# Uniform operand offsets, the attention mask as a TensorE product, and softmax scaling on ScalarE

## The chip, the cores and the metric

The kernel runs on one core of a Trainium2 chip. The metric is device time in microseconds (us) of the whole kernel, the median of three runs. TensorE (PE in the profile; PEld is its weight load) does the products, VectorE (DVE) and ScalarE (ACT) do element-wise work, GpSimd (POOL) some of it and a few transfers, SyncE (SP) issues the others.

## The reference

The reference is one layer of a diffusion block for 256 latent and 256 context tokens of width 2048. Cut to what matters:

```python
h  = modulate(rms_norm(x, norm_attn_w), sh_a, sc_a)        # shift, scale and gate come from silu(c) @ w_ada + b_ada
hc = modulate(rms_norm(ctx, norm_attn_w), csh_a, csc_a)
q, k, v, u = split_projection(h @ w_in)                     # 16 query heads, 4 key heads of 64
qc, kc, vc, uc = split_projection(hc @ w_in)
# latent window attention: each query sees latent keys at most 128 away, all 256 context keys and a sink logit
s_win = where(abs(qpos - kpos) <= 128, q @ k.T / 8, -1e30)
p = softmax(concat([s_win, q @ kc.T / 8, sink]))            # the sink's share is dropped
attn = p_win @ v + p_ctx @ vc
x = x + g_a * (concat([attn, multiscale_pool(u)]) @ w_out)
hm = modulate(rms_norm(x, norm_mlp_w), sh_m, sc_m)
x = x + g_m * (square(relu(hm @ w_mlp_up)) @ w_mlp_down)    # hidden width 8192
out = rms_norm(x, final_norm_w)
```

All data are float32.

## The kernel before

Every large product is split in two parts per operand: hi is the operand rounded to the type fp32r, lo is the rest. `mm3` adds three products (hi x hi, hi x lo, lo x hi) in one bank of PSUM. Weights come in tiles of 128 x 2048 numbers through a ring of five buffers (`raw`, class `WeightStream`); `split_to` makes their parts in halves of 128 x 1024: ScalarE casts `hi`, VectorE subtracts `lo`, in rings of six. The activations have the same two parts: `hhi` and `hlo` for the input projection (`modulated`), `mx` (both parts in one tile) for the output projection and the up product, `ahi` and `alo` for the down product (`activation`). The line of a product in the profile is that of `mm3` (290, 291, 292), of `up_group` (920) or of the attention.

The stages follow each other: modulation and input projection (to about 207 us), attention with the last input projections, the pooling mixer and some modulation products (`ps_ada`) mixed in (207 to about 315), output projection (`ps_w`), norm, then the MLP in turns: two up groups (`ps_up`), then a down stretch (`ps_d`).

Attention goes through 16 units: a pair of heads and a block of 128 queries. The 512 keys of a unit are 256 latent and 256 context keys. For each of its two heads, `scores` makes a bank of 128 x 512 scores by two products; the mask concerns 128 of its columns. `maxima` adds the mask on VectorE and takes the row maxima; `exponentials` makes the exponentials and their sums on ScalarE; `normalize` adds the sink's share to the sums, inverts them and scales the probabilities `p` on VectorE; `transpose` turns `p` on TensorE (`tp_p`) and ScalarE copies the result to `pT`; `attend` multiplies it with the values (`ps_o`). The loop writes, for step n: scores of unit n, `attend`, transposes of unit n - 2, maxima of n, normalization of n - 1, exponentials of n. A scheduler then sets each engine's order from that program; each engine runs its own list strictly in that order and waits at its head.

`gap` allocates a few bytes that nothing uses, so that the tiles behind it begin elsewhere. The places below are the first byte of a tile in each partition of SBUF, as a remainder by 512 (128 float32 numbers, one row of a weight tile of 128 columns).

Of the kernel before, what the change touches and what calls it, by code (L numbers as in the profile page):

```python
# [9 lines left out]
F32R = mybir.dt.float32r  # L10
I32 = mybir.dt.int32
AF = mybir.ActivationFunctionType
ALU = mybir.AluOpType
AX = mybir.AxisListType

P = 128
# [33 lines left out]
def gap(pool, n, name="gap"):  # L50

    pool.tile([P, n // 4], F32, tag=name, name=name, bufs=1)


class WeightStream:
# [28 lines left out]
    def split_to(self, n):  # L88
        nc = self.nc
        while self.n_half < min(n, len(self.halves)) and not self.hold:  # L90
            i, h = self.halves[self.n_half]
            if i >= self.n_load:
                break
            raw = self.raw[i][:, 2 * h : 2 * h + 2, :]
            hi = self.pool.tile([P, 2, 512], F32R, tag="hi", name="hi", bufs=N_HALF)
            if not self.n_half:
                gap(self.pool, 320)
            lo = self.pool.tile([P, 2, 512], F32R, tag="lo", name="lo", bufs=N_HALF)
            up = nc.scalar.copy(hi, raw)  # L99
            low = nc.vector.tensor_tensor(lo, raw, hi.bitcast(F32), ALU.subtract)  # L100
            self.last = (up.ins, low.ins)
            self.split[i, h] = (hi, lo)
            self.n_half += 1
# [23 lines left out]
def kernel(  # L127
# [314 lines left out]
    def modulated(c_, streams=(0, 1)):  # L442

        pool = hpb if c_ in (2, 3, 6, 7) else hpa
        if 0 in streams:
            hhi = pool.tile([P, 2, 512], F32R, tag="hhi", name="hhi", bufs=2)
            if c_ in (0, 2):
                gap(pool, 320, "gaph")
            hlo = pool.tile([P, 2, 512], F32R, tag="hlo", name="hlo", bufs=2)
            hparts[c_] = hhi, hlo  # L450
        hhi, hlo = hparts[c_]
        for j in range(2):
            k = 2 * c_ + j
            xk = xT[k // 4][:, k % 4, :]
            for s in streams:
                v = xk[:, T * s : T * s + T]
                nc.vector.tensor_scalar(v, v, am_a[:, k, s : s + 1], sm_a[:, k, s : s + 1], ALU.mult, ALU.add)
            ts_ = slice(T * streams[0], T * streams[-1] + T)
            up = nc.scalar.copy(hhi[:, j, ts_], xk[:, ts_])
            low = nc.vector.tensor_tensor(hlo[:, j, ts_], xk[:, ts_], hhi[:, j, ts_].bitcast(F32), ALU.subtract)  # L460
            hs[k] = lambda s, j=j: (hhi[:, j, s], hlo[:, j, s])
        return up.ins, low.ins
# [122 lines left out]
    for op in in_ops:  # L585
        if op[0] == "ctx":
            with tc.issue_after(first_split[0]), tc.issue_after(first_split[1]):
                normalize(2)
                normalize(3)
            modulated(0, (1,))  # L590
            xn_es.close()
            mixa = ctx.enter_context(tc.tile_pool(name="mixa", bufs=1, side="left", reuse_waits="tile"))
            gap(mixa, 192)
            hpb = hpb_es.enter_context(tc.tile_pool(name="hpb", bufs=1, side="left", reuse_waits="tile"))
            gap(hpb, 192)
        else:
            run_in(op)
    gap(hpa, 320)
    st_es.close()
    hpa_es.close()  # L600

# [5 lines left out]
    def parts(j):  # L607
# [17 lines left out]
                            fill=MASKED, base=0, channel_multiplier=1)  # L625
    nc.gpsimd.affine_select(out=mask[:, 1, :], in_=mask[:, 1, :], pattern=[[1, P]], compare_op=ALU.is_ge,
                            fill=MASKED, base=0, channel_multiplier=-1)

    swap = [(i + 16) % 32 for i in range(32)]

# [76 lines left out]
    class Unit:  # L707
# [4 lines left out]
        def scores(self):  # L712
            khi, klo = kparts[self.cc // 2]
            self.s = []
            for i in range(2):
                ps = bank("ps_s")
                q = qparts[self.cc, i][:, P * self.qb : P * self.qb + P]
                nc.tensor.matmul(ps, q, khi, start=True, stop=False)
                nc.tensor.matmul(ps, q, klo, start=False, stop=True)
                self.s.append(ps)  # L720

        def maxima(self):

            st = atp.tile([P, 4, 2], F32, tag="st", name="st", bufs=6)
            mx, self.sum, self.es, self.nm = (st[:, i, :] for i in range(4))
            for i, ps in enumerate(self.s):
                far = ps[:, P : 2 * P] if self.qb == 0 else ps[:, 0:P]
                nc.vector.tensor_tensor(far, far, mask[:, self.qb, :], ALU.add)
                nc.vector.reduce_max(mx[:, i : i + 1], ps, axis=AX.X)
            nc.vector.scalar_tensor_tensor(self.nm, mx, -0.125, nsink[:, self.heads], ALU.mult, ALU.min)  # L730
            nc.vector.tensor_tensor(self.es, sink[:, self.heads], self.nm, ALU.add)
# [8 lines left out]
        def normalize(self):  # L740
            nc.vector.tensor_tensor(self.sum, self.sum, self.es, ALU.add)
            nc.vector.reciprocal(self.sum, self.sum)
            for i in range(2):
                p = self.p[:, i, :]
                nc.vector.tensor_scalar(p, p, self.sum[:, i : i + 1], None, ALU.mult)

        def transpose(self):
            if self.qb == 0:
# [49 lines left out]
    for n in range(len(units) + 3):  # L798
        if n < 16:
            if n % 4 == 0:  # L800
                split_keys(n // 4)
            units[n].scores()
        fill_to((n + 0.5) / 17)
        if n >= 4 and n % 2 == 0:
            attend((n - 4) // 2)
        if 2 <= n < 18:
            units[n - 2].transpose()
        if n < 16:
            units[n].maxima()
        if 1 <= n < 17:  # L810
            units[n - 1].normalize()
        if n < 16:
            units[n].exponentials()
            if n % 2 == 0 and n < 14:
                split_queries(n // 2 + 1)
        fill_to((n + 1) / 17)
# [71 lines left out]

    def activation(pss):
        ahi = mp.tile([P, 4, T], F32R, tag="ahi", name="ahi", bufs=3)  # L890
        gap(mp, 64)
        alo = mp.tile([P, 4, T], F32R, tag="alo", name="alo", bufs=3)
        for m in range(4):
            t = mp.tile([P, T], F32, tag="act", name="act", bufs=2)
            if pss[m].shape[1] == T:
                nc.scalar.activation(t, pss[m], AF.Relu)
                nc.vector.tensor_tensor(t, t, t, ALU.mult)
            else:
                nc.scalar.copy(t, pss[m][:, T : 2 * T])
                nc.vector.tensor_tensor(t, pss[m][:, 0:T], t, ALU.add)  # L900
                nc.vector.scalar_tensor_tensor(t, t, 0.0, t, ALU.max, ALU.mult)
            nc.scalar.copy(ahi[:, m, :], t)
            nc.vector.tensor_tensor(alo[:, m, :], t, ahi[:, m, :].bitcast(F32), ALU.subtract)
        return ahi, alo
# [198 lines left out]
```

## Time and profile before

| | us |
|---|---|
| median of three runs | 1156.07 (1155.22 to 1157.96) |
| the profiled execution, whole | 1154.18 |
| its span, from the first to the last instruction | 1152.4 |
| TensorE busy | 1109.2 (96%) |
| VectorE busy | 801.9 (70%) |
| ScalarE busy | 504.9 (44%) |
| GpSimd busy | 35.5 (3%) |

Busy shares are averages over stages with different limits. A TensorE product is counted until its modelled end, so products in close order overlap, and the distance of their starts says more than their duration. A line such as `out<-in` names the tiles of an instruction without buffer numbers; `x` is a count.

### The profile page before, as it was taken

To read this page: it belongs to the slowest core of one execution; us is meant where nothing else is said; L and a number is where in the kernel's file an instruction comes from. 1 tells how busy PE (TensorE), PEld (TensorE's weight loads), DVE (VectorE), ACT (ScalarE), POOL (GpSimd) and SP (SyncE) were. 2 spreads that over 40 slices of the span, in tenths; PEclk is the share of its full clock that TensorE was granted. 3 is DMA by queue.
4 is the path that set the end of the run, shared out by engine and by line. 5 is a ranking of instruction groups with operands and counts; after the bars stand their busy time and mean duration, and the time that the engine had idled before them with its cause. 6 is when DMAs were issued, how large, how long until landed. Compare 5 with 4: busy or idle time off the path is not lost.

```text
span 1152.4 us, 16086 instructions
## 1 busy us (share of the span) xinstructions
PE 1109.2 (96%) x6332; PEld 903.4 (78%) x6332; DVE 801.9 (70%) x1286; ACT 504.9 (44%) x762; POOL 35.5 (3%) x53
## 2 busy tenths in 40 slices
PE   4999999979999989999999999999999999999996
PEld 3767778746578869988888888888888888888885
DVE  5655557988787888796775774784664665587576
ACT  4623233377634443365433444433444443443452
POOL 1000001610000000000000000000000000000000
PEclk9999999999999989999999999999999999999998
DMA  9999897667897999977775775676556556556532
GB/s 341 358 342 345 274 332 265 212 237 272 278 380 266 311 324 343 354 257 248 272 247 184 255 268 197 239 260 205 186 189 200 192 183 184 192 188 203 183 110 74
DMA packets 174012, 286.66 MB, mean 249 GB/s; under 512 B 5608, under 2 KB 72352, under 8 KB 172784
## 3 DMA queue, kind: packets, MB, share of 16 engines
q1 hardware_dynamic: 172800, 279.55, 72.4%
q0 software_dynamic: 848, 5.55, 1.3%
q8 instruction: 50, 0.82, 0.3%
q10 hardware_dynamic: 288, 0.52, 0.1%
q14 instruction: 26, 0.21, 0.1%
HBM read 283.50 MB, written 2.10 MB: 248 GB/s over the span
## 4 chain that ended last, share of the span: by engine, by line
PE 80%; DVE 9%; DMA 6%; ACT 2%; issue 1%; SPq 0%; POOL 0%; ACTq 0%; DVEq 0%
PE ps_up L920 25%; PE ps_d L290 10%; PE ps_d L291 10%; PE ps_d L292 10%; PE ps_ada L307 5%; DMA raw<-in_w_mlp_up_dram 3%; DVE lo L100 3%; PE ps_qu L290 2%; PE ps_qu L292 2%; PE ps_qu L291 2%; DVE ada_v L329 1%; PE ps_o L764 1%; PE ps_w L290 1%; PE ps_w L292 1%; PE ps_w L291 1%
## 5 line engine op out<-in xcount | busy, mean ns | idle before, releaser
L100 DVE TENSOR_TENSOR lo<-raw,hi 128x1024 fp32r<-128x1024 f32 x330 | 396.9, 1224 | 210.4 <-ACT hi L99 203.8
L99 ACT CAST hi<-raw 128x1024 fp32r<-128x1024 f32 x330 | 337.7, 1050 | 414.5 <-PE ps_up L920 150.6
L290 PE MATMUL ps_d<-hi,ahi 128*128 128x512 f32 (+1 forms) x520 | 202.8, 391 | 0.0
L291 PE MATMUL ps_d<-lo,ahi 128*128 128x512 f32 (+1 forms) x520 | 202.3, 390 | 0.0
L920 PE MATMUL ps_up<-mx,hi 128*128 128x512 f32 x832 | 200.0, 392 | 0.0
L292 PE MATMUL ps_d<-hi,alo 128*128 128x512 f32 (+1 forms) x520 | 199.8, 388 | 0.0
L920 PEld LDWEIGHTS ps_up<-mx,hi 128*128 128x128 f32 x832 | 153.4, 188 | 31.8 <-issue 1.9
L292 PEld LDWEIGHTS ps_d<-hi,alo 128*128 128x128 f32 x520 | 97.7, 188 | 22.4
L290 PEld LDWEIGHTS ps_d<-hi,ahi 128*128 128x128 f32 x520 | 97.8, 188 | 21.7
L291 PEld LDWEIGHTS ps_d<-lo,ahi 128*128 128x128 f32 x520 | 97.7, 188 | 20.7
L329 DVE SCALAR_TENSOR_TENSOR ada_v<-raw,c_sil,ada_v 128x512 f32<-128x512 f32 x135 | 100.8, 747 | 14.7 <-DMA raw<-in_w_ada_dram 13.1
L920 PEld LDWEIGHTS ps_up<-mx,lo 128*128 128x128 f32 x832 | 105.3, 189 | 4.0
L920 PE MATMUL ps_up<-mx,lo 128*128 128x256 f32 x832 | 106.6, 281 | 0.0
L307 PE MATMUL ps_ada<-raw,c_sil 128*32 128x512 f32 x480 | 70.8, 625 | 0.9 <-DMA raw<-in_w_ada_dram 0.9
L290 PE MATMUL ps_qu<-hhi,hi 128*128 128x256 f32 x240 | 69.8, 292 | 1.4 <-ACT hi L99 1.4
L292 PE MATMUL ps_qu<-hhi,lo 128*128 128x256 f32 x240 | 67.4, 284 | 0.3 <-DVE lo L100 0.3
L291 PE MATMUL ps_qu<-hlo,hi 128*128 128x256 f32 x240 | 67.3, 281 | 0.0
L290 PEld LDWEIGHTS ps_qu<-hhi,hi 128*128 128x128 f32 x240 | 45.4, 189 | 16.6 <-issue 9.2
L290 PE MATMUL ps_up<-mx,hi 128*128 128x256 f32 x192 | 54.0, 290 | 1.6 <-ACT mx L885 1.5
L291 PE MATMUL ps_up<-mx,hi 128*128 128x256 f32 x192 | 53.5, 283 | 0.0
L292 PE MATMUL ps_up<-mx,lo 128*128 128x256 f32 x192 | 52.4, 283 | 0.0
L290 PE MATMUL ps_w<-hi,mx 128*128 128x512 f32 x128 | 51.4, 402 | 0.0
(199 smaller groups left out, 1323.1 us busy)
## 6 DMA issues: line engine op xcount, KB each, us to landing
raw<-in_w_ada_dram SPq DMA_DIRECT2D x128, 512.0 KB, 7.5
raw<-in_w_mlp_up_dram SPq DMA_DIRECT2D x64, 1024.0 KB, 5.4
raw<-in_w_mlp_down_dram SPq DMA_DIRECT2D x64, 1024.0 KB, 5.1
raw<-in_w_ada_dram SPq DMA_DIRECT2D x32, 1024.0 KB, 6.2
raw<-in_w_in_dram SPq DMA_DIRECT2D x19, 1024.0 KB, 7.6
raw<-in_w_out_dram SPq DMA_DIRECT2D x16, 1024.0 KB, 7.8
xnat<-in_x_dram SPq DMA_DIRECT2D x2, 1024.0 KB, 6.0
xnat<-in_ctx_dram SPq DMA_DIRECT2D x2, 1024.0 KB, 11.6
```

The source lines that it names most:

```text
L99: up = nc.scalar.copy(hi, raw)
L100: low = nc.vector.tensor_tensor(lo, raw, hi.bitcast(F32), ALU.subtract)
L290: nc.tensor.matmul(ps, a[0], b[0], start=first, stop=False, skip_group_check=True)
L291: nc.tensor.matmul(ps, a[0], b[1], start=False, stop=False, skip_group_check=True)
L292: nc.tensor.matmul(ps, a[1], b[0], start=False, stop=last, skip_group_check=True)
L307: nc.tensor.matmul(ps[32 * j : 32 * j + 32, :], c_sil[:, 4 * kg + j, :], raw[:, j, :], start=(kg == 0), stop=(kg == 3), tile_position=(0, ...
L329: nc.vector.scalar_tensor_tensor(box["e"], raw[:, j, :], sc, box["e"], ALU.mult, ALU.add)
L764: nc.tensor.matmul(ps[64 * i : 64 * i + 64, 0:T], va[k // 2][:, k % 2, 64 * g : 64 * g + 64], pT[:, k, i, :], start=(k == 0), stop=(k == 3 ...
L920: nc.tensor.matmul(ps, wk, h, start=part == k == 0, stop=part == 1 and k == KC - 1, skip_group_check=True)
```

## The change

Offsets. The gaps between `hi` and `lo`, between `hhi` and `hlo`, and in front of `mx` go; the gap between `ahi` and `alo` moves behind `alo`. `hhi` and `hlo` get one tag for each of their two buffers, in the same turn as before. The places change so (remainder by 512):

| tile | before | after |
|---|---|---|
| `hi` (weights) | 160 | 160 |
| `lo` (weights) | 480 | 160 |
| `hhi` | 352 | 352 |
| `hlo` | 160 | 352 |
| `mx` | 160 | 160 |
| `ahi` | 416 | 416 |
| `alo` | 480 | 416 |

In the down product `hi` and `lo` are streamed (the moving operand) and `ahi` and `alo` are the weights loaded into the array; in the up product it is the other way, `mx` is streamed and `hi` and `lo` are loaded. By 2048 the remainder of `mx` goes from 1696 to 1184, that of `hi` is 1184 in both.

Mask. Two copies in fp32r, `mask_r` and `ident_r`, are made once on ScalarE. Behind the two score products a third one, identity times mask, adds the mask to its 128 columns of the bank; VectorE's add is gone. Normalization: the probabilities are scaled by ScalarE. The loop writes the normalization of unit n - 1 ahead of the maxima of unit n.

```diff
@@ split_to
             hi = self.pool.tile([P, 2, 512], F32R, tag="hi", name="hi", bufs=N_HALF)
-            if not self.n_half:
-                gap(self.pool, 320)
             lo = self.pool.tile([P, 2, 512], F32R, tag="lo", name="lo", bufs=N_HALF)
@@ modulated
-            hhi = pool.tile([P, 2, 512], F32R, tag="hhi", name="hhi", bufs=2)
-            if c_ in (0, 2):
-                gap(pool, 320, "gaph")
-            hlo = pool.tile([P, 2, 512], F32R, tag="hlo", name="hlo", bufs=2)
+            hhi = pool.tile([P, 2, 512], F32R, tag=f"hhi{c_ % 2}", name="hhi", bufs=1)
+            hlo = pool.tile([P, 2, 512], F32R, tag=f"hlo{c_ % 2}", name="hlo", bufs=1)
@@ pools
-            gap(mixa, 192)
...
-    gap(hpa, 320)
+    gap(hpa, 128)
@@ masks
+    mask_r = atp.tile([P, 2, P], F32R, name="mask_r")
+    ident_r = atp.tile([P, P], F32R, name="ident_r")
+    nc.scalar.copy(mask_r, mask)
+    nc.scalar.copy(ident_r, ident)
@@ scores
-                nc.tensor.matmul(ps, q, khi, start=True, stop=False)
-                nc.tensor.matmul(ps, q, klo, start=False, stop=True)
+                nc.tensor.matmul(ps, q, khi, start=True, stop=False, skip_group_check=True)
+                nc.tensor.matmul(ps, q, klo, start=False, stop=False, skip_group_check=True)
+                far = ps[:, P : 2 * P] if self.qb == 0 else ps[:, 0:P]
+                nc.tensor.matmul(far, ident_r, mask_r[:, self.qb, :], start=False, stop=True, skip_group_check=True)
@@ maxima
-                far = ps[:, P : 2 * P] if self.qb == 0 else ps[:, 0:P]
-                nc.vector.tensor_tensor(far, far, mask[:, self.qb, :], ALU.add)
@@ normalize
-                nc.vector.tensor_scalar(p, p, self.sum[:, i : i + 1], None, ALU.mult)
+                nc.scalar.activation(p, p, AF.Copy, scale=self.sum[:, i : i + 1])
@@ the loop over units
+        if 1 <= n < 17:
+            units[n - 1].normalize()
         if n < 16:
             units[n].maxima()
-        if 1 <= n < 17:
-            units[n - 1].normalize()
@@ activation
         ahi = mp.tile([P, 4, T], F32R, tag="ahi", name="ahi", bufs=3)
+        alo = mp.tile([P, 4, T], F32R, tag="alo", name="alo", bufs=3)
         gap(mp, 64)
-        alo = mp.tile([P, 4, T], F32R, tag="alo", name="alo", bufs=3)
```

The scheduler's lists of the two kernels differ in the attention stage and in a few places of the output projection and norm; the order of transfers is the same.

VectorE, second and third unit (the second unit's probabilities are `p_2231`, the third's `p_2325`; their small columns are `st_2220` and `st_2314` before, `st_2226` and `st_2320` after; `ps_s_2263` and `ps_s_2266` or `ps_s_2267` are the third unit's scores), before:

```order
L728 TENSOR_TENSOR ps_s_2263<-ps_s_2263,mask_1825 128x128
L728 TENSOR_TENSOR ps_s_2266<-ps_s_2266,mask_1825 128x128
L741 TENSOR_TENSOR st_2220<-st_2220 128x2
L729 TENSOR_REDUCE st_2314<-ps_s_2263 128x1
L729 TENSOR_REDUCE st_2314<-ps_s_2266 128x1
L742 RECIPROCAL st_2220<-st_2220 128x2
L438 TENSOR_TENSOR ua3_278<-ps_qu_2269,ua3_278 128x2x256
L730 SCALAR_TENSOR_TENSOR st_2314<-st_2314,nsink_1823 128x2
L745 TENSOR_SCALAR p_2231<-p_2231,st_2220 128x512 x2
```

and after:

```order
L740 TENSOR_TENSOR st_2226<-st_2226 128x2
L728 TENSOR_REDUCE st_2320<-ps_s_2263 128x1
L728 TENSOR_REDUCE st_2320<-ps_s_2267 128x1
L741 RECIPROCAL st_2226<-st_2226 128x2
L729 SCALAR_TENSOR_TENSOR st_2320<-st_2320,nsink_1819 128x2
L730 TENSOR_TENSOR st_2320<-sink_1817,st_2320 128x2
L436 TENSOR_TENSOR ua3_278<-ps_qu_2271,ua3_278 128x2x256
L740 TENSOR_TENSOR st_2320<-st_2320 128x2
L741 RECIPROCAL st_2320<-st_2320 128x2
```

(Line numbers of the changed kernel are one or two lower here.) The third unit's mask adds and the second unit's scalings are gone from this list. The second unit's reciprocal still stands behind the third unit's two maxima, and the third unit's own reciprocal now follows within a few rows.

ScalarE, a little later (`p_2325` as above, `p_2376` is the fourth unit's; `pT_2301` before and `pT_2303` after is the transposed copy of the first two units, `tp_p` the banks it empties), before:

```order
L737 ACTIVATE p_2325,st_2314<-ps_s_2263,st_2314 128x512
L737 ACTIVATE p_2325,st_2314<-ps_s_2266,st_2314 128x512
L755 COPY pT_2301<-tp_p_2302 128x4x128
L755 COPY pT_2301<-tp_p_2308 128x4x128
L735 ACTIVATE st_2314<-st_2314 128x2
L660 CAST qs0_2446<-qa1_272 64x256
L648 CAST khi_2649<-ka1_280 64x512
L649 CAST khi_2649<-ka1_280 64x512
L660 CAST qs1_2449<-qa1_272 64x256
L313 COPY ada_e_2404<-ps_ada_2212 128x512
L755 COPY pT_2301<-tp_p_2353 128x4x128
L755 COPY pT_2301<-tp_p_2359 128x4x128
```

and after:

```order
L754 COPY pT_2303<-tp_p_2304 128x4x128
L754 COPY pT_2303<-tp_p_2310 128x4x128
L659 CAST qs0_2446<-qa1_272 64x256
L744 ACTIVATE p_2325<-p_2325,st_2320 128x512 x2
L647 CAST khi_2649<-ka1_280 64x512
L648 CAST khi_2649<-ka1_280 64x512
L659 CAST qs1_2449<-qa1_272 64x256
L736 ACTIVATE p_2376,st_2371<-ps_s_2340,st_2371 128x512
L736 ACTIVATE p_2376,st_2371<-ps_s_2344,st_2371 128x512
L754 COPY pT_2303<-tp_p_2355 128x4x128
L734 ACTIVATE st_2371<-st_2371 128x2
L754 COPY pT_2303<-tp_p_2361 128x4x128
```

The scalings of the third unit (`p_2325<-p_2325`) are new here, and those of the second stand a few rows further up; both pairs come ahead of the last copies into `pT`, and the fourth unit's exponentials do too.

TensorE, from the second unit's transposes to the first product with the values (`ps_s_2392` and its partner are scores of the fifth unit, `ps_o` the product with the values), before:

```order
L307 MATMUL ps_ada_2212<-raw_2126,c_sil_75 32x512 x4
L307 MATMUL ps_ada_2212<-raw_2213,c_sil_75 32x512 x4
L753 MATMUL tp_p_2353<-ident_64,p_2231 128x128 x4
L753 MATMUL tp_p_2359<-ident_64,p_2231 128x128 x4
L718 MATMUL ps_s_2392<-khi_2386,qs0_2329 128x512
L719 MATMUL ps_s_2392<-klo_2387,qs0_2329 128x512
L718 MATMUL ps_s_2395<-khi_2386,qs1_2332 128x512
L719 MATMUL ps_s_2395<-klo_2387,qs1_2332 128x512
L764 MATMUL ps_o_2406<-pT_2301,va0_281 64x256
```

and after:

```order
L305 MATMUL ps_ada_2214<-raw_2128,c_sil_75 32x512 x3
L752 MATMUL tp_p_2355<-ident_64,p_2231 128x128 x4
L752 MATMUL tp_p_2361<-ident_64,p_2231 128x128 x4
L305 MATMUL ps_ada_2214<-raw_2128,c_sil_75 32x512
L717 MATMUL ps_s_2392<-khi_2386,qs0_2329 128x512
L718 MATMUL ps_s_2392<-klo_2387,qs0_2329 128x512
L720 MATMUL ps_s_2392<-mask_r_1829,ident_r_1830 128x128
L717 MATMUL ps_s_2396<-khi_2386,qs1_2332 128x512
L718 MATMUL ps_s_2396<-klo_2387,qs1_2332 128x512
L720 MATMUL ps_s_2396<-mask_r_1829,ident_r_1830 128x128
L305 MATMUL ps_ada_2214<-raw_2215,c_sil_75 32x512 x4
L763 MATMUL ps_o_2408<-pT_2303,va0_281 64x256
```

One product with the mask stands directly behind each pair of score products, and some of the modulation products (`ps_ada`) that stood ahead of the transposes stand behind them and behind the scores.

## Rows read from the trace of the kernel before

**Rows 1.** The page: busy time by engine; slices of TensorE and its clock.

```profile
PE 1109.2 (96%) x6332; PEld 903.4 (78%) x6332; DVE 801.9 (70%) x1286; ACT 504.9 (44%) x762; POOL 35.5 (3%) x53
...
PE   4999999979999989999999999999999999999996
...
PEclk9999999999999989999999999999999999999998
```

**Rows 2.** Attention by windows: us, busy (x count) by engine, TensorE clock, DMA share, GB/s.

```profile
222.00:242.00 20.00, 14.32 (x99) 8.80 (x97) 19.75 (x45) 11.40 (x30) 9.60 (x12) 1.00 0.58 215
242.00:262.00 20.00, 18.67 (x118) 8.76 (x118) 16.96 (x50) 14.42 (x35) 0.00 (x0) 1.00 0.70 231
262.00:282.00 20.00, 20.00 (x145) 12.84 (x144) 17.84 (x54) 15.13 (x41) 0.00 (x0) 1.00 0.69 250
282.00:309.00 27.00, 26.09 (x175) 15.35 (x170) 20.78 (x55) 20.32 (x47) 0.00 (x0) 1.00 0.77 270
207.00:309.00 102.00, 93.06 (x631) 58.03 (x632) 89.99 (x231) 64.04 (x159) 19.54 (x23) 1.00 0.67 235
```

**Rows 3.** TensorE's waits from 200 to 320: us in total, times, longest.

```profile
PE ps_o L764 <- ACT pT L755: 3.4, 2, 2.5
PE tp_p L753 <- DVE p L745: 3.2, 2, 1.8
...
PE tp_p L753 <- ACT pT L755: 0.8, 1, 0.8
```

**Rows 4.** Timeline of TensorE, 225 to 243; idle before and releaser in brackets.

```profile
225.61 1.09 PE L753 MATMUL tp_p<-ident,p 128*128 128x128 f32 x8
...
231.24 0.63 PE L753 MATMUL tp_p<-ident,p 128*128 128x128 f32 x4 [1.76 <-DVE p L745]
...
236.72 0.65 PE L764 MATMUL ps_o<-pT,va 128*64 128x256 f32 x2 [2.53 <-ACT pT L755]
...
242.87 0.30 PE L753 MATMUL tp_p<-ident,p 128*128 128x128 f32 x1 [1.48 <-DVE p L745]
```

**Rows 5.** Timeline of TensorE: start and end of a down stretch.

```profile
831.03 0.75 PE L920 MATMUL ps_up<-mx,lo 128*128 128x256 f32 x5
831.63 0.40 PE L290 MATMUL ps_d<-hi,ahi 128*128 128x512 f32 x1
...
876.01 1.30 PE L920 MATMUL ps_up<-mx,hi 128*128 128x512 f32 x5
```

**Rows 6.** Windows for one line: a down stretch (line 290), the up stretch behind it (line 920).

```profile
831.63:876.01 44.38, 25.27 (x64) 11.91 (x64) 1.00 0.60 188
...
876.01:920.31 44.30, 44.30 (x256) 39.11 (x255) 1.00 0.59 192
```

**Rows 7.** The page's costliest groups: count, busy us, mean ns, idle before.

```profile
L290 PE MATMUL ps_d<-hi,ahi 128*128 128x512 f32 (+1 forms) x520 | 202.8, 391 | 0.0
L291 PE MATMUL ps_d<-lo,ahi 128*128 128x512 f32 (+1 forms) x520 | 202.3, 390 | 0.0
...
L292 PE MATMUL ps_d<-hi,alo 128*128 128x512 f32 (+1 forms) x520 | 199.8, 388 | 0.0
```

**Rows 8.** VectorE's groups by line: count, busy us, mean ns, idle before.

```profile
L745 DVE TENSOR_SCALAR p<-p,st 128x512 f32<-128x512 f32 x32 | 15.1, 512 | 0.2
...
L728 DVE TENSOR_TENSOR ps_s<-ps_s,mask 128x128 f32<-128x128 f32 x32 | 8.7, 292 | 4.7 <-PE ps_s L719 4.4
```

**Rows 9.** Tiles `st` and `p`: ns min/median/max.

```profile
L730 DVE SCALAR_TENSOR_TENSOR st<-st,nsink x16: 147/151/2057, 215.4 to 300.0; 128x2 f32<-128x2 f32 x16
...
L745 DVE TENSOR_SCALAR p<-p,st x32: 472/480/1480, 223.1 to 304.3; 128x512 f32<-128x512 f32 x32
```

**Rows 10.** Line 1029: ns min/median/max.

```profile
L1029 ACT ACTIVATE x<-x,rs_y x5: 705/707/722, 1141.9 to 1146.8; 128x512 f32<-128x512 f32 x5
```

**Rows 11.** The chain that ended last, 200 to 320: start, us, step.

```profile
228.68 1.98 DVE st L730
```

**Rows 12.** Windows for line 745 (VectorE's scalings).

```profile
222.00:242.00 20.00, 3.66 (x6) 1.00 0.58 215
```

## Prediction

> **What bounds the kernel now.** I read the page's busy shares and slices first: TensorE is busy for 1109.2 of 1152.4 us, almost every slice from the second on shows a 9 for it, and its granted clock is at full speed nearly throughout [rows 1]. So time can come off in two ways only: TensorE's products follow each other more closely, or its few waits go. The table by stretches then shows where waits are possible: in the attention stage, 207 to 309 us, TensorE is busy for 93.06 of 102 us, and the shortfall lies mostly in 222 to 242 (14.32 of 20), where VectorE is busy for 19.75 of 20 [rows 2]. From 242 on TensorE is nearly full (18.67, 20.00, 26.09 of 20, 20 and 27). The list of waits names them: TensorE waited 3.2 us for the normalized probabilities from VectorE, 3.4 us for the transposed ones from ScalarE, 0.8 us for a bank that ScalarE was emptying, 7.4 us in all [rows 3]. The timeline has the three long ones, at 231.24, 236.72 and 242.87 [rows 4]. Everything after the stage is products in close order: a down stretch takes 876.01 - 831.63 = 44.38 us [rows 5] and holds 64 products of each of three kinds [rows 6], so 44.38 / 192 = 231 ns for each product of 512 columns. The next up stretch is 44.30 us for 256 products, 128 of 512 columns and 128 of 256 [rows 6]; five of the latter begin 831.63 - 831.03 = 0.60 us before the down stretch, so 0.12 us each [rows 5], which leaves (44.30 - 128 x 0.12) / 128 = 0.226 us for one of 512 columns.
>
> **Part 1: the offsets.** Nothing is computed differently; only tiles lie elsewhere. The direct hint is in the three lines of the down products: mean 391 ns (hi times ahi), 390 (lo times ahi), 388 (hi times alo) [rows 7]. The ends are modelled, but the three differ by the same rule. The third kind is the one whose follower streams from the same offset (hi, then the next hi); behind the first two the streamed operand jumps between 160 and 480. After the change all three stay at 160, and the weights loaded meanwhile lie at 416 throughout, as behind the third kind now. I take the third kind's duration for all three: 3 + 2 = 5 ns a triple, 520 triples [rows 7], 2.6 us less. Bounds: no gain, if the 3 ns belong to the place in the triple and not to the address; at best the up stretch's pace, (231 - 227) ns x 1560 = 6.2 us; at worst all three at the slowest line, 1 + 3 = 4 ns x 520 = 2.1 us more. In the up groups the lo weights move from 480 to 160. The hi weights of the same groups already lie at 160 with the streamed activations at 160, and these are the fastest products of 512 columns above, so I take nothing there; bounds 3 ns either way on 832 products, 2.5 us. The input and output projections (some 1,400 products) change in the same way; I have no row that sets their kinds apart, so nothing, with the smaller difference above as a bound, 1 ns each, 1.4 us.
>
> A rule speaks against this part: the Trainium skill (TensorE: Matmul & The Clock Gate, Step-by-step: what each phase is for) has two independent read ports for streamed operand and weights, so that loading the next weights takes no read bandwidth from the running product. By it addresses would not matter and this part's sum would be 0; the trace has only the 3 ns of 391 against it, and that rule is the reason for the third rival.
>
> **Part 2: mask on TensorE.** 32 products of 128 columns are added, one behind each pair of score products (the order shows it directly behind them). Nearest row: eight transposes of 128 columns took 1.09 us, 0.136 each with the last one's tail [rows 4]; from below, a quarter of a 512-column product, 231 / 4 = 58 ns. I take 0.11, nearer to the transposes, since they too load 128 columns of weights for 128 streamed: 32 x 0.11 = 3.5 us (1.9 to 4.4), on TensorE, which is the bound behind 242. VectorE loses 32 adds of 292 ns [rows 8]. The two copies that make the mask and identity operands stand once on ScalarE, well before the scores, where the stage before leaves it idle: nothing.
>
> **Part 3: normalization on ScalarE.** VectorE loses 32 x 0.51 = 16.3 us by the mean of its line, and 15.1 by its busy time [rows 8]. These instructions were also stretched: the median is 480 ns, the longest 1480, and the small instruction that makes the exponents' bias has 151 and 2057 [rows 9], while GpSimd worked on the pooling in the same stretch (9.60 of 20 us in 222 to 242 [rows 2]). ScalarE gains 32 scalings; the nearest row is its scaling of 512 columns by a column of scalars at the end of the kernel, 707 ns [rows 10]: 22.6 us. Here too a rule speaks against the change: the Trainium skill (ScalarE: Activation LUTs, Rules for kernel authors) sends multiplications to VectorE. By engine time the rows agree, 707 against 480 ns; by which engine is late in 222 to 242 they do not.
>
> What this does to the waits. Up to the reciprocal of the second unit VectorE drops six mask adds (6 x 0.29) and a pair of scalings (2 x 0.47), 2.7 us, and the chain of waits has the third unit's bias there, 1.98 us for a small instruction, on VectorE as well [rows 11]. So the second unit's probabilities come 4 us or more earlier, and TensorE's waits for VectorE (3.2) and for the bank (0.8) go: 4.0 us. The wait at 236.72 for ScalarE's transposed copy mostly stays: ScalarE starts earlier, but in the changed order it has two pairs of scalings (4 x 0.707 = 2.8 us) ahead of that copy; I take 0.9 off the 3.4. Behind 242 ScalarE is short: it is busy 14.42 + 15.13 + 20.32 = 49.87 of 67 us [rows 2], idle 17.1, and gets the scalings that VectorE now does from there on, 32 - 6 [rows 12], so 26 x 0.707 = 18.4. TensorE can run ahead a little, because the next transposes are two units behind, and the splits of the output weights can slip into the next stage; I put 1.0 us of new waits there.
>
> **Part 4: sums ahead of the next maxima.** This is written order only; in the built order the reciprocal of the second unit still stands behind the third's maxima, which no longer wait for mask adds. Nothing beyond part 3. DMA engines are at 0.58 to 0.77 in this stage [rows 2], so earlier consumption can be fed.
>
> **Sum.** Offsets -2.6; waits -4.0 - 0.9; mask products +3.5; new waits +1.0: -3.0 us. The profiled execution took 1154.18 us, 1.78 outside its span and 1.89 below the median of the three runs; on it the sum gives 1151.2, on the median 1156.07 - 3.0 = **1153.1 us**. A measurement of this kernel can tell about 0.2% (2.3 us) from no change.
>
> **Rivals.**
> *ScalarE becomes the bound (ends slower).* In 242 to 309 it would need 49.87 + 18.4 = 68.3 us of 67 without any waiting. If half of its former idle time was waiting for exponents' biases and products that still come in turn, 8.6 us, the stretch grows by 1.3 + 8.6 = 9.9 us, which hides the 26 mask products in it; with the earlier waits gone (-4.9) and six mask products in front (+0.7) the stage is 5.7 us longer, with the offsets' -2.6 the kernel +3.1: 1159.2. It decides from about 8 us of such waiting on. For it: the sum of busy times. Against: the splits can slip, and ScalarE waited because VectorE was late.
> *Equal offsets cost (slower).* Now streamed operand and weights meet at one offset in more pairs: +2.1 in the down groups, +2.5 in the up groups, attention -0.4: +4.2, 1160.3. For it: a tile's offset may matter either way. Against: the up groups' hi products.
> *The offsets do nothing (no change).* Only attention's -0.4 is left: 1155.7. For it: 3 ns of 391 is little, and the order within the triple could make it.
> *More of both (faster).* The down products fall to the up groups' pace (-6.2), all 7.4 us of waits go, mask products +3.5: -10.1, 1146.0.
>
> **How the numbers follow.** Forecast 0.31, more of both 0.14, offsets do nothing 0.28, ScalarE bound 0.19, equal offsets cost 0.08. The forecast lies 0.7 us beyond the bound of 2.3, so I put 0.23 of it under faster and 0.08 under no change. Of "offsets do nothing" 0.06 go to faster, 0.19 to no change, 0.03 to slower; of the two slower ones, 3.1 and 4.2 us above the median, 0.15 and 0.06 to slower, 0.04 and 0.02 to no change. That makes faster 0.23 + 0.14 + 0.06 = 0.43, same 0.33, slower 0.24. The range takes in the rivals at both ends as far as 8 in 10 need: 1146 to 1159.5; the forecast's own is 1150 to 1156.
>
> **What would show it.** Right: a down stretch of 192 products near 44.0 us instead of 44.38; TensorE's waits for probabilities gone in 222 to 243 and those for the transposed copy left; ScalarE nearly without idle time in 242 to 309; the first output product 0 to 1 us earlier than now. Wrong: down stretches unchanged or longer; TensorE waiting for ScalarE by several us behind 242; mask products that stand 0.2 us apart or delay the weights behind them.

## The result, and the profile after

The changed kernel takes 1147.05 us (median of five runs, 1143.71 to 1149.24), the kernel before 1155.8 in the same comparison (five runs, 1153.46 to 1157.96). The ratio is 0.9924, with an interval of 0.9904 to 0.9945: 8.8 us less, between 6.4 and 11.1. Forecast were 3.0 less.

The page of the changed kernel, the lines that answer to [rows 1]:

```profile
PE 1104.6 (96%) x6364; PEld 909.3 (79%) x6364; DVE 779.2 (68%) x1222; ACT 523.6 (46%) x796; POOL 37.0 (3%) x53
...
PE   4999999999999989999999999999999999999996
...
PEclk9999999999999989899999999999999999999998
```

TensorE has 32 instructions more and is busy for 4.6 us less, at the same clock. So its products stand closer. The three kinds of down product on the same page, for [rows 7]:

```profile
L288 PE MATMUL ps_d<-hi,ahi 128*128 128x512 f32 (+1 forms) x520 | 200.0, 386 | 0.0
L289 PE MATMUL ps_d<-lo,ahi 128*128 128x512 f32 (+1 forms) x520 | 200.0, 386 | 0.0
L290 PE MATMUL ps_d<-hi,alo 128*128 128x512 f32 (+1 forms) x520 | 198.7, 386 | 0.0
```

And the windows of a late down stretch and of the up stretch behind it, with the columns of [rows 6]:

```profile
826.89:870.44 43.55, 24.91 (x64) 11.90 (x64) 1.00 0.60 190
...
870.44:914.95 44.51, 44.51 (x256) 39.29 (x255) 1.00 0.59 193
```

All three kinds now have one mean, and it is lower than that of each of the three before. A down stretch is 44.38 - 43.55 = 0.83 us shorter; an up stretch is 44.51 - 44.30 = 0.21 us *longer*.

In attention, the waits of TensorE (for [rows 3]) and the windows (for [rows 2]):

```profile
PE ps_o L763 <- ACT pT L754: 4.7, 4, 1.8
PE ps_s L717 <- DVE qs L660: 0.9, 2, 0.5
PE ps_ada L305 <- ACT p L736: 0.2, 1, 0.2
```

```profile
222.00:242.00 20.00, 18.24 (x125) 12.18 (x124) 16.41 (x38) 16.26 (x41) 9.65 (x12) 1.00 0.60 212
242.00:262.00 20.00, 20.00 (x141) 9.72 (x141) 12.01 (x32) 18.43 (x44) 0.00 (x0) 1.00 0.93 330
262.00:282.00 20.00, 18.70 (x136) 12.09 (x134) 12.29 (x38) 19.87 (x49) 0.00 (x0) 1.00 0.56 202
282.00:309.00 27.00, 25.12 (x170) 16.38 (x167) 13.71 (x32) 23.39 (x50) 0.00 (x0) 1.00 0.77 266
```

The waits for VectorE's probabilities and for the bank are gone, those for ScalarE's copy grew from 3.4 to 4.7 us. From 242 to 282 VectorE has room now (12.01 and 12.29 of 20 us) and ScalarE is the full engine (18.43 and 19.87).

Where the time went, from the first starts of each kind of product (score `ps_s`, output `ps_w`, up `ps_up`, down `ps_d`) in the timelines (us; the last column ends with the last product):

| kernel | first score to first output product | to first up product | to first down product | to the end |
|---|---|---|---|---|
| before | 101.8 | 111.1 | 75.0 | 646.9 |
| changed | 100.2 | 108.4 | 77.9 | 641.8 |
| offsets only | 102.6 | 109.9 | 74.0 | 641.8 |
| attention only | 102.4 | 109.4 | 77.2 | 646.9 |

The last column is the clean part: 5.1 us less with the new offsets, nothing without them. In the input projection ahead of this table (first key product to first score) the new offsets save another 1.4 us (156.8 to 155.4). The first three columns move by about a microsecond from execution to execution: a kernel that differs from before in the down products alone (experiment 4) has 102.7, 111.6 and 74.7.

### The profile page after: what moved, and what is told of

Read it like the earlier page. It is cut to its first block, busy times and chain, and to the rows that moved or that the text cites. A ratio compares the mean times of both kernels' runs of the same rounds, so it can differ in the third digit from the quotient of the medians.

```text
span 1145.3 us, 16131 instructions
## 1 busy us (share of the span) xinstructions
PE 1104.6 (96%) x6364; PEld 909.3 (79%) x6364; DVE 779.2 (68%) x1222; ACT 523.6 (46%) x796; POOL 37.0 (3%) x53
## 4 chain that ended last, share of the span: by engine, by line
PE 88%; DVE 4%; ACT 3%; DMA 3%; issue 1%; SPq 0%; ACTq 0%; DVEq 0%
PE ps_up L919 25%; PE ps_d L288 10%; PE ps_d L289 10%; PE ps_d L290 10%; PE ps_ada L305 4%; PE ps_w L288 3%; PE ps_w L290 3%; PE ps_w L289 3%; PE ps_qu L288 2%; PE ps_qu L290 2%; PE ps_qu L289 2%; PE ps_up L288 1%; DVE lo L98 1%; PE ps_o L763 1%; PE ps_up L289 1%; PE ps_up L290 1%
## 5 line engine op out<-in xcount | busy, mean ns | idle before, releaser
L288 PE MATMUL ps_d<-hi,ahi 128*128 128x512 f32 (+1 forms) x520 | 200.0, 386 | 0.0
L289 PE MATMUL ps_d<-lo,ahi 128*128 128x512 f32 (+1 forms) x520 | 200.0, 386 | 0.0
L327 DVE SCALAR_TENSOR_TENSOR ada_v<-raw,c_sil,ada_v 128x512 f32<-128x512 f32 x135 | 100.9, 748 | 12.7 <-DMA raw<-in_w_ada_dram 11.1
L305 PE MATMUL ps_ada<-raw,c_sil 128*32 128x512 f32 x480 | 68.3, 628 | 2.2 <-DMA raw<-in_w_ada_dram 1.9
```

The costliest lines, as they stand in the source:

```text
L288: nc.tensor.matmul(ps, a[0], b[0], start=first, stop=False, skip_group_check=True)
L289: nc.tensor.matmul(ps, a[0], b[1], start=False, stop=False, skip_group_check=True)
L305: nc.tensor.matmul(ps[32 * j : 32 * j + 32, :], c_sil[:, 4 * kg + j, :], raw[:, j, :], start=(kg == 0), stop=(kg == 3), tile_position=(0, ...
L327: nc.vector.scalar_tensor_tensor(box["e"], raw[:, j, :], sc, box["e"], ALU.mult, ALU.add)
```

## The experiments

Every ratio is to the kernel before, run beside it on the same chip. The experiments come from four chips, so they are compared by these ratios. Two theories at the start. **Places**: how closely products follow each other depends on where their operands lie, and this brings nearly everything. **Attention**: the freed waits bring most, and the offsets at most the 2.6 us of the forecast. The spacing of products is given as the mean distance between the start of one product and the start of the next in the trace, over all of a kind (504 for each kind of down product), without distances over 30 ns above the median.

**1 and 2. The two halves of the change.** `off_only` is the kernel before with the hunks of the diff on `split_to`, `modulated`, the pools and `activation`; `att_only` has the others.

```diff
 off_only:   -  gap(self.pool, 320)  -  gap(pool, 320, "gaph")  -  gap(mixa, 192)
             +  gap(hpa, 128)        +  alo ahead of gap(mp, 64)
 att_only:   +  mask_r, ident_r and the third product in scores
             +  nc.scalar.activation(p, p, AF.Copy, scale=...)   +  normalize ahead of maxima
```

> The kernel before with all changes of offsets and nothing else. Place theory (the distance of a product to the next depends on where its operands lie): the down products stand 227 ns apart as in the changed kernel, a late down stretch takes 43.55 us (44.38 before), a late up stretch 44.5 (44.3 before), the output projection loses 2 to 3 us, and the whole is 5 to 7 us under the kernel before. Rival (attention brings most of the 8.7 us, and the shorter products only show there because of it): at most 2.6 us, the term of the forecast.

> The kernel before with the changes in attention (mask on TensorE, scaling on ScalarE, loop order) and the old offsets. Place theory: from the first score to the output projection 1.5 to 2 us less (102 us before), down and up stretches as before (44.38 and 44.30), the whole 1 to 2 us under the kernel before. Rival (attention brings most): 5 us or more.

`off_only` 1149.41 us, ratio 0.9928 (0.9911 to 0.9945), 8.3 us less, where 5 to 7 were expected; `att_only` 1157.04 us, 0.9996 (0.9986 to 1.0006), nothing, where 1 to 2 us less were expected. The product of the two is 0.9924, the ratio of the whole change. The theory of attention falls. The down and up stretches of `off_only` are those of the changed kernel (us, TensorE busy, weight loads, VectorE, ScalarE, clock, DMA share, GB/s), those of `att_only` those of before.

```profile
826.14:869.69 43.55, 43.55 (x192) 35.87 (x192) 4.73 (x7) 0.00 (x0) 1.00 0.60 190
...
869.69:914.19 44.50, 44.50 (x256) 39.31 (x255) 1.59 (x4) 1.64 (x5) 1.00 0.58 192
```

**3 and 4. One tile at a time.**

```diff
 lo160:      lo = self.pool.tile([P, 2, 512], F32R, tag="lo", ...)     # now ahead of the gap
             if not self.n_half:
                 gap(self.pool, 320)
 alo_only:   alo = mp.tile([P, 4, T], F32R, tag="alo", ...)            # now ahead of the gap
             gap(mp, 64)
```

> The kernel before with the tile lo at 160 (by 512) instead of 480, nothing else moved. The forecast's step (the jump of the streamed operand between 160 and 480 costs 3 and 2 ns in the first two of a triple): the triple falls from 693.5 to 688 ns, a late down stretch to 44.05 us. Rival (the place of the loaded weights 416 and 480 is what costs): triple unchanged, 44.38. Up stretch: 44.3 if the 256-column products depend on the place of mx, 44.5 as in the changed kernel if on the place of lo.

> The kernel before with alo at 416 instead of 480, nothing else moved. The forecast's step: no change, a late down stretch 44.38 us. Rival (the place of the loaded weights costs): it falls to 43.6 us by itself. If both places count, each of the two single moves gives a part, and the sum of the parts is 0.83 us a stretch.

1155.9 us, 0.9995 (0.9982 to 1.0009), and 1157.1 us, 1.0007 (0.9995 to 1.0018): neither does anything. The down products of `lo160`, in the costliest groups of its page:

```profile
L292 PE MATMUL ps_d<-hi,alo 128*128 128x512 f32 (+1 forms) x520 | 202.5, 393 | 0.0
L291 PE MATMUL ps_d<-lo,ahi 128*128 128x512 f32 (+1 forms) x520 | 201.5, 389 | 0.0
L290 PE MATMUL ps_d<-hi,ahi 128*128 128x512 f32 (+1 forms) x520 | 200.4, 387 | 0.0
```

and of `alo_only`:

```profile
L290 PE MATMUL ps_d<-hi,ahi 128*128 128x512 f32 (+1 forms) x520 | 202.5, 391 | 0.0
L291 PE MATMUL ps_d<-lo,ahi 128*128 128x512 f32 (+1 forms) x520 | 202.3, 390 | 0.0
L292 PE MATMUL ps_d<-hi,alo 128*128 128x512 f32 (+1 forms) x520 | 201.2, 391 | 0.0
```

By starts, the three kinds stand 232.5, 231.5 and 229.6 ns apart before, 228.9, 229.5 and 235.0 with `lo` moved, 231.6, 232.0 and 232.5 with `alo` moved: triples of 693.6, 693.4 and 696.1 ns. With both moved it is 226.9, 226.7 and 226.9, 680.5. The 688 ns expected of `lo160` by the forecast's step did not come, nor did part of the gain with either single move: with `lo` moved the first two kinds gain what the third loses, with `alo` moved the third loses more than the first gains, and only the two together bring 13 ns. That a late down stretch of `alo_only` would not get shorter was expected by the forecast's step; it is even 0.2 us longer (44.55). The up stretch of `lo160` is 44.52 us, as in the changed kernel, though `mx` is where it was: there it is the place of `lo` that costs 0.2 us.

**5 and 6. Is it that the places are equal, or which they are?**

```diff
 aft_a480:   +  gap(mp, 64)          # now ahead of ahi: ahi and alo at 480, not 416
 aft_mx352:  +  gap(mixa, 192)       # mx at 352, not 160
             -  gap(hpb, 192)
```

> The changed kernel with ahi and alo both at 480 instead of 416, nothing else moved: uniform again, but at another distance from the streamed hi and lo. If being uniform is what matters, the three down products stay at 227 ns and a late down stretch at 43.55 us. Rival (it was 416 that suited): up to 235 ns as in the mixed case, 44.4 us and more.

> The changed kernel with the tiles mx at 352 (by 512) instead of 160, nothing else moved but the two small tiles ga and gm. In the up stretches the streamed operand then lies 192 behind the loaded weights, as in the input projection of the changed kernel. Distance theory (what counts for a settled run of 256-column products is the distance of the two operands): they come 116.5 ns apart instead of 120, a late up stretch 44.1 us or less (44.5), the whole 4 to 5 us under the changed kernel. Rival (the input projection is quicker for another reason): 120 ns and 44.5 us, no change. 512-column products: 227 by both.

`aft_a480`: 1157.53 us, 1.0009 (0.9998 to 1.0021): all of the gain is lost, with the loaded tiles as uniform as in the changed kernel. `aft_mx352`: 1146.15 us, 0.9917 (0.9905 to 0.9930). Windows for the down products of `aft_a480` (us, TensorE busy, weight loads, VectorE):

```profile
831.66:876.47 44.81, 44.81 (x192) 35.91 (x192) 4.73 (x7) 0.00 (x0) 1.00 0.59 186
```

and the up products of `aft_mx352` by line and form:

```profile
L919 PE MATMUL ps_up<-mx,hi 128*128 128x512 f32 x832 | 204.0, 397 | 0.0
...
L919 PE MATMUL ps_up<-mx,lo 128*128 128x256 f32 x832 | 103.3, 277 | 0.0
```

The down products of `aft_a480` stand 233.3 ns apart, all three. So uniform is not enough: 416 suited and 480 does not. With `mx` at 352 the 256-column products come at 114.3 ns (119.6 in the changed kernel), as the theory of the distance said, but the 512-column ones go from 228.3 to 233.1, which it had not said. In both runs 512-column products whose streamed operand lies 192 behind the loaded one, by 512, take 233. The whole moved by less than the interval tells, where 4 to 5 us less were expected.

**7 and 8. The two halves of attention**, each taken out of the changed kernel.

```diff
 aft_maskdve:  -  third product in scores, mask_r, ident_r
               +  nc.vector.tensor_tensor(far, far, mask[:, self.qb, :], ALU.add)
 aft_normdve:  -  nc.scalar.activation(p, p, AF.Copy, scale=...)
               +  nc.vector.tensor_scalar(p, p, self.sum[:, i : i + 1], None, ALU.mult)
```

> The changed kernel with the mask added by VectorE again (scaling stays on ScalarE, loop order too). By the forecast's terms the 32 mask products (3.5 us) go, VectorE gets 32 adds of 0.29 us back but is not full any more: 1 to 3.5 us under the changed kernel. Rival (attention's time is set by ScalarE or by the transfers of weights behind it): within 1 us of the changed kernel.

> The changed kernel with the probabilities scaled by VectorE again (mask stays on TensorE, loop order too). By the forecast's terms ScalarE loses 32 x 0.72 us and TensorE's waits for the transposed copy (4.7 us) shrink to 3, while one or two waits for VectorE (1 to 2 us) come back: within 2 us of the changed kernel. Rival (ScalarE is what sets attention now): 3 us or more under it.

`aft_maskdve`: 1150.41 us, 0.9949 (0.9937 to 0.9961), by the medians slower than the changed kernel (0.9924, 0.9904 to 0.9945), where 1 to 3.5 us less were expected; the two intervals overlap. `aft_normdve`: 1144.72 us, 0.9903 (0.9890 to 0.9916), by the ratios 2.4 us under the changed kernel, between the 2 of the expectation and the 3 of its rival. TensorE's waits from 200 to 320 in the first:

```profile
PE ps_o L758 <- ACT pT L749: 9.5, 3, 4.9
PE ps_ada L305 <- DVE ga L528: 1.7, 1, 1.7
```

and in the second:

```profile
PE tp_p L752 <- DVE p L744: 1.6, 2, 0.9
PE ps_s L717 <- DVE qs L660: 1.0, 2, 0.6
PE ps_o L763 <- ACT pT L754: 0.9, 1, 0.9
```

With the new offsets there are now four versions: neither edit 0.9928, mask alone 0.9903, scaling alone 0.9949, both 0.9924. By these ratios the mask on TensorE is worth 2.9 us and the scaling on ScalarE costs 2.4, and the two nearly cancel. Neighbouring intervals overlap; clear is the difference between 7 and 8, 5.3 us. The traces, one execution each, do not add up so: from the first score to the first down product they have 286.5 us with neither edit, 286.1 with the mask alone, 290.3 with the scaling alone and 286.4 with both. What the mask alone gains up to the first output product (98.0 us against 102.6) is gone again by the end of the first up stretch. So it is not shown that the mask brings anything without the scaling. That the scaling costs has a third pair for it, experiments 6 and 10.

**9. Alternating streams at good distances.** `nd_` kernels have the scaling on VectorE, as 8.

```diff
 nd_lo416:  +  gap(self.pool, 256)             # ahead of lo, and another behind it: lo at 416
```

> The changed kernel with the scaling on VectorE and with lo at 416 (by 512) instead of 160, nothing else moved by 512. The streams of a down triple alternate again, 160 and 416, against weights at 416, so at distances 256 and 0, which are both quick where all products of a run have them. Distance theory: 227 ns stay, a late down stretch 43.55 us. Rival (a stream that alternates costs, whatever its distances): 231 ns, 44.3 us. The up stretch's 256-column products get the distance 256, which no run has yet: below 120 ns it would be a gain, up to 2 us on the whole.

1144.2 us, 0.9888 (0.9872 to 0.9904). The windows for the down products and for the up products behind them:

```profile
825.81:869.36 43.55, 43.55 (x192) 35.85 (x192) 4.72 (x7) 0.00 (x0) 1.00 0.60 190
...
869.36:913.86 44.50, 44.50 (x256) 39.29 (x255) 1.59 (x4) 1.64 (x5) 1.00 0.58 192
```

The streams alternate between 160 and 416, as far apart by 512 as can be, and the products still stand 226.7 to 227.0 ns apart: a jump of 256 costs nothing. What fits is the distance of the streamed operand from the loaded one: 256 and 0 are equally good. That no jump costs anything is not shown: in experiment 4 the stream jumps between 160 and 480 while all loaded tiles lie at 416, and the triple takes 696.1 ns; in the changed kernel, without that jump, it takes 680.5. If places count by 256, then 160 and 416 are one place, and this experiment has no jump at all. The 256-column products do not profit from 256: 119.6.

**10 and 11. The best of the single runs together, and one more distance.**

```diff
 nd_mx352:  as 6 and 8 together
 nd_mx288:  +  gap(mixa, 128)        # mx at 288
            -  gap(hpb, 192)
            +  gap(hpb, 64)
```

> The changed kernel with the scaling on VectorE and mx at 352. By the two single runs: 0.8 us less in the MLP's later part, so 1144 us or a little less, if the shorter products of the first up stretch bring nothing because transfers set its end; 2 us more if they do.

> The changed kernel with the scaling on VectorE and mx at 288, so that in the up stretches the streamed operand lies 128 behind the loaded weights, the one distance in steps of 64, taken by 256, that no run has in settled products. Distance theory (the spacing depends on the distance, by 256): between its neighbours, 229 to 233 ns for 512 columns and 115 to 117 for 256, a late up stretch 44.2 to 44.4 us, and the whole within 2 us of the kernel with mx at 352. Rival (only mx at 352 or 160 as such counts): 227 and 120 ns, 44.5 us. Down stretches unchanged, 43.55 us, by both.

`nd_mx352`: 1142.79 us, 0.9885 (0.9873 to 0.9898), the shortest median of all, though the interval overlaps those of 8 and 9, with the first up stretch 1.5 us shorter than in 8 (75.8 against 77.3). Experiment 6 differs from it in the scaling alone and has 0.9917 (0.9905 to 0.9930): on ScalarE the scaling costs 3.7 us here, and the intervals do not meet. The traces agree, with 286.5 and 283.7 us from the first score to the first down product. `nd_mx288`: 1146.59 us, 0.9917 (0.9894 to 0.9940), by the ratios 3.7 us above it, where 2 were the bound, though the intervals just overlap: its 512-column products at 232.7 ns are as expected, its 256-column ones at 118.7 are not (115 to 117 expected). The windows for the up products of the two:

```profile
866.48:910.87 44.39, 44.39 (x256) 38.56 (x255) 1.59 (x4) 1.56 (x5) 1.00 0.58 194
```

```profile
868.38:913.36 44.98, 44.98 (x256) 39.22 (x255) 1.58 (x4) 1.64 (x6) 1.00 0.58 190
```

**12. What lengthens the first up stretch?** It is 2.9 us longer in the changed kernel, 2.2 in `att_only`.

```diff
 nd_halfup:  S.add("w", (lambda t: t[:, 0:2, :], w_up_v[:, 4 * kg : 4 * kg + 2, ...]))   # first 12 tiles
             h0 = 0 if i in self.once else h
             raw = self.raw[i][:, 2 * h0 : 2 * h0 + 2, :]
```

> The changed kernel with the scaling on VectorE; of the 12 weight tiles of the first up stretch only the first half is transferred (6 MB less) and used twice, so this part of the computation is another; TensorE, VectorE and ScalarE do the same instructions. Theory (transfers set the end of the first up stretch): the stretch falls from 77.3 us to 73 or less, and the first down product comes 3 us or more earlier, counted from the first key product. Rival (TensorE's order or VectorE sets it): within 1 us of 441.5.

1146.79 us, 0.9921 (0.9909 to 0.9933), no gain. This kernel leaves out half of the first stretch's weights and uses the other half twice. The windows of the first up stretch of `aft_normdve` and of `nd_halfup` (columns as in [rows 2]):

```profile
414.83:492.09 77.26, 75.07 (x605) 74.62 (x601) 63.96 (x95) 32.79 (x43) 0.00 (x0) 0.96 0.93 320
```

```profile
412.49:492.74 80.25, 74.31 (x602) 73.84 (x601) 65.00 (x97) 32.66 (x42) 0.00 (x0) 0.96 0.74 247
```

The DMA engines fall from 0.93 to 0.74 and the stretch gets longer by about what it starts earlier; from the first key product to the first down product it is 441.0 us, 441.5 in `aft_normdve`. Halving the transfers of its weights does not end it earlier, and the theory falls in this form. The chain of waits of the changed kernel shows VectorE ahead of the end, with the last modulation columns and the splits of weights in one list:

```profile
472.28 2.35 DVE lo L98 x2
474.63 0.67 DVE ada_v L327
475.44 1.14 PE ps_adac L335 x8
477.00 0.50 DVE x2T L882
477.52 0.52 ACT mx L884
478.08 1.65 PE ps_up L288 x6
```

Transfers stand in these chains too. In the kernel before, four transfers of up weights take 31 us of the chain between 405 and 500; in the changed kernel one of them is left, 8.62 us from 452.35 on; and in `nd_halfup` a transfer of modulation weights, which come through the same ring, stands right ahead of the last modulation columns:

```profile
467.67 7.79 DMA raw<-in_w_ada_dram
```

So this end may be set by VectorE's list or by the modulation weights. No run here took either away, and it stays open.

## Why the prediction was right, and where its steps failed

The direction was right, and the time lies in the range, 1 us above its lower end. The size was off by a factor of three: the forecast's own range, 1150 to 1156, was missed, and the stated one reaches to 1147 only because it takes in the rival *More of both*. By the medians the gain came out of one part alone.

**Part 1, the offsets: the step that failed.** Forecast were 2.6 us less, measured 8.3 less (6.4 to 10.3). The prediction read from the 391, 390 and 388 ns of [rows 7] that the third kind is free of a loss since its follower streams from the same offset, and gave its duration to all three. But the third kind was slowed as well, 229.6 ns by starts before and 226.9 after: every kind fell to 227 ns, 13 ns a triple in place of 5, and the eight down stretches became 6.5 us shorter by their starts. That is the bound "at the up stretch's pace" (6.2), which stood in the text and was put into a rival with 0.14. And the jump of the stream, the reason given, is not the whole of it. Without any jump the triple takes 693.4 ns in experiment 3 and 700 in experiment 5; with a jump of 256 it takes 680.6 in experiment 9. Only beside loaded tiles that all lie at 416 does the old jump make the difference, 696.1 against 680.5 (experiment 4 and the changed kernel). So the places of both operands count together, and the step priced the stream's alone. The up groups were put at nothing: they became 1.4 us longer in the later stretches, inside the bound of 2.5, since `lo` at 160 lies at distance 0 from `mx`. The projections were put at nothing with a bound of 1 ns a product: in the input projection 672 products of 256 columns came 2 ns closer each (118.5 to 116.3, 1.4 us by the stage), the output projection's 384 came 4.6 closer (232.0 to 227.4, 1.8 us).

The rule of the Trainium skill (TensorE: Matmul & The Clock Gate, Step-by-step: what each phase is for), two independent read ports, would have made this part 0. The trace does not agree: the same products take from 226.9 to 233.3 ns by the place of their operands alone, and the measurement decides.

**Parts 2 and 3: the sum right, partly by luck, and the two edits not told apart.** Forecast were 0.4 us less for attention, measured 0.5 less (from 1.6 less to 0.7 more). The waits for VectorE and for the bank went as forecast (4.0 us). The wait for ScalarE's copy was put at 3.4 - 0.9 plus 1.0 of new waits, 3.5; it is 4.7. The long one fell from 2.53 to 1.76 us, about as forecast; behind 242 there are three, 1.10, 0.83 and 1.06 us, where there was one of 0.91, so 2.1 us are new there. The mask products cost about what was forecast: the next product starts 58 ns behind one of them, a score product that follows one takes 283 ns in place of 231, and from the first score product of a head to the product behind the group it is 610 ns in place of 514 (means over the 32 groups without those with a wait): 0.096 us each, 3.1 us in all, 3.5 forecast. By these terms of the trace the sum is -4.0 - 0.8 + 3.1 + 2.1 = +0.4, so luck has a share in the agreement. And the prediction has no price for each edit: it took 1.7 us of mask adds and 0.9 of scalings off VectorE's list ahead of the second unit's reciprocal, and let both earn the freed waits. Experiments 7 and 8 set them apart: by the medians the changed kernel is slower without the mask edit and faster without the scaling edit (0.9949 and 0.9903 against 0.9924). The likely reason, argued and not shown: an add of 0.29 us on VectorE stood ahead of the maxima, on the way to the exponentials, so its removal shortens the chain of each unit; the scaling went from an engine with 512 ns for it to one with 725, into the same list as the exponentials and the transposed copies. The rule of the Trainium skill (ScalarE: Activation LUTs, Rules for kernel authors) that sends multiplications to VectorE agrees with this kernel: the scaling takes 512 ns on VectorE and 725 on ScalarE, and on ScalarE it costs 2.4 to 3.7 us of the whole by the three pairs.

**Part 4** was rightly put at nothing: the built order is the same, row for row on TensorE, VectorE and ScalarE, if the loop of the changed kernel is written in the old order.

**The rivals.** *ScalarE becomes the bound* did not come: it is busy for 61.7 of 67 us behind 242, not 68.3 needed. Experiment 7 comes nearest to that rival: with the mask on VectorE again TensorE waits 9.5 us for ScalarE's copies. *Equal offsets cost* was true of the up groups alone. *The offsets do nothing* falls. *More of both* named the place and the size of the down products' gain, but the waits for ScalarE did not go.

**What the profile was to show.** A down stretch near 44.0 us: 43.55. The first output product 0 to 1 us earlier: 309.3 - 307.1 = 2.2, of which 0.6 lie ahead of attention. TensorE's waits for the copy behind 242: 3.0 us together, 2.1 of them new, where 1.0 was forecast as new.

## What to carry to other kernels

Where products in close order bound a kernel, the place of the two operands in a partition is worth measuring, and as a pair: each of two single moves did nothing here, and both together gave 13 ns in 694. Equal places are not the aim; try the distance of streamed and loaded tile in steps of 64 bytes, for each product width apart. When an edit moves two operations off a full engine, run each alone: here the whole of the two was nothing (0.9996), while the kernels with one of them differ by 5.3 us.

## What was not expected of the hardware

The spacing of products in settled runs, by the distance of the streamed from the loaded operand (place of one less place of the other, taken by 256, since 0 and 256 gave the same: 226.8 and 119.6 ns):

| distance | 512 columns, ns | 256 columns, ns |
|---|---|---|
| 0 | 227 (up), 226.8 (down, places 160 or 416 against 416) | 119.9, 119.6 |
| 64 | 227.0 to 230.2 (output projection of 6 and 10, 160 against 352) | 116.5 to 117.1 |
| 128 | 232.7 | 118.7 |
| 192 | 233.1 (up, 352 against 160), 233.3 (down, 160 against 480) | 114.3 to 116.4 |

What is best for one width is not best for the other: 0 for 512 columns, 192 for 256. The table is not a law: the 256-column products of the kernel before lie at 192 too (160 against 480) and take 118.0, and no run has steps finer than 64. Mixed distances cost more than their mean: `lo160` has 0, 0 and 192, for which the table gives 227 + 227 + 233 = 687 ns, and takes 693.4; `alo_only` has 0, 64 and 0, at most 684 by the table, and takes 696.1. A change of pattern also has a tail: in each up group the first five 512-column products stand about 233, 235, 229, 232 and 230 ns apart, and from the sixth on 227, before and after alike. Why the places matter no run here shows.
